# One-level Strassen products for the MLP up-projections of a two-layer trunk, with the MLP split into an up and a down phase

## The chip, the cores and the metric

The kernel is one program on one core of a Trainium2 chip. The metric is device time in microseconds (us). Before the change three runs took 2766.5, 2768.09 and 2774.47 us, median 2768.09. TensorE is PE in the profile (its weight loads PEld), VectorE is DVE, ScalarE is ACT, GpSimd is POOL, and SP is the engine that issues most loads.

## The reference

A sequence of 1024 tokens with 1024 features goes through two layers. Layer 0 mixes tokens by retention, layer 1 by a state-space block (S5). After each mixer comes the same MLP, and everything is float32:

```python
def conv_ffn(h, w_up, conv_w, conv_b, w_down):        # D_FF = 2816
    val, gate = jnp.split(h @ w_up, 2, axis=-1)       # (1024 x 1024) @ (1024 x 5632)
    gate = causal_depthwise_conv(gate, conv_w, width=3) + conv_b
    return (jax.nn.silu(gate) * val) @ w_down
h = rms_norm(x) * (1.0 + sc2) + sh2
x = x + g2 * conv_ffn(h, ...)
```

## The kernel before

Activations lie with features on the 128 partitions and tokens along the row. A float32 product is made of three reduced-precision ones (`mm3`): weight and activation are each split into a high part `hi` and a rest `lo`, and one bank of PSUM takes hi·hi, hi·lo and lo·hi. The split of a weight tile is one ACT copy (`hi`, L214) and one DVE subtraction (`lo`, L215).

A half is 512 of the 1024 tokens, and all matmuls of the MLP are 128x128 weights against 128x512 activations. The 2816 hidden features are 22 tiles. For each tile, `up` (L1352) makes gate and value for both halves, 8 blocks of the reduction each: 2 x 2 x 8 x 3 = 96 matmuls. `gate_out` copies the gate into the buffer `E`, `val_out` runs the convolution (one DVE `tensor_scalar`, two `scalar_tensor_tensor`), the silu on ACT, the product with the value (L1345), and splits the result again (L1349, L1350). After every two tiles the down-projection of the two tiles before them is added to `x` in SBUF (L1189). `lead` (L1363) begins an MLP: its first 96 matmuls need half 0 alone, while the normalisation of half 1 (`Norm.steps`) comes in piece by piece, block after block of the reduction.

Each engine executes its own queue in the order in which the Python code issues instructions. `W` (`Stream`) holds the weights in order of use: raw tiles (3 buffers), then hi and lo (5 buffers each). `pump` splits one tile ahead wherever it is called. `bg` takes one step of background work: in layer 0's MLP this is `s5_weights`, which prepares tables for S5, mainly on POOL, in 201 steps; 25 of them make eight groups of S5 (two half-blocks).

Of the kernel before, what the change touches and what calls it, by code (L numbers as in the profile page):

```python
# [18 lines left out]
P = 128  # L19
T = 1024  # L20
# [61 lines left out]
def trunk_kernel(ctx: ExitStack, tc: tile.TileContext, x, c, pos, ada_w, ada_b, ret_w_in, ret_w_out,  # L82
# [85 lines left out]
    NB = NFF // 2  # L168

    def ffn_list(l):  # L170
        wu, wd = ffn_w_up[l], ffn_w_down[l]
        for b in range(NB + 1):
            if b < NB:
                for ff in (2 * b, 2 * b + 1):
                    yield ("ug", l, ff), cols8(wu, FF + ff * P), 8
                    yield ("uv", l, ff), cols8(wu, ff * P), 8
            if b == NB:
                dn = range(2 * NB - 4, 2 * NB)
            elif 0 < b < NB - 1:
                dn = range(2 * b - 2, 2 * b)  # L180
            else:
                dn = ()
            for ff in dn:
                yield ("dn", l, ff), wd[ff * P:(ff + 1) * P, :].rearrange("p (o n) -> p o n", o=1), 1

    class Stream:
        RAW = 3
        BUFS = 5

        def __init__(self):  # L190
            self.items = list(weight_list())
            self.raw, self.hl = {}, {}
            self.nd = self.nsp = self.ng = self.use = 0

        def loads(self, upto=None):
            top = min(self.nsp + self.RAW, len(self.items))
            if upto is not None:
                top = min(top, upto)
            while self.nd < top:
                _, ap, k = self.items[self.nd]  # L200
# [4 lines left out]

        def split(self, later=None):
            i = self.nsp
            if i not in self.raw:
                self.loads()
            r = self.raw.pop(i)  # L210
            _, _, k = self.items[i]
            hi = w_p.tile([P, T], F32R, tag="whi", name="whi", bufs=self.BUFS)
            lo = w_p.tile([P, T], F32R, tag="wlo", name="wlo", bufs=self.BUFS)
            A.activation(out=hi, in_=r, func=AF.Copy)  # L214
            low = lambda: V.tensor_tensor(out=lo, in0=r, in1=f(hi), op=ALU.subtract)  # L215
            low() if later is None else later.append(low)
            self.hl[i] = (hi.rearrange("p (k n) -> p k n", k=k), lo.rearrange("p (k n) -> p k n", k=k))
            self.nsp += 1

        def get(self, key, n=1, more=False):  # L220
# [1606 lines left out]
```

## Time and profile before

| what | value |
|---|---|
| runs | 2766.5, 2768.09, 2774.47 us |
| span of the profiled execution | 2763.6 us |
| PE busy | 2701.4 us, 98% |
| DVE busy | 1568.2 us, 57% |
| ACT busy | 778.7 us, 28% |
| POOL busy | 769.4 us, 28% |
| DMA moved | 288.39 MB, mean 104 GB/s |

The span is from the first to the last instruction of one profiled execution; its own device time is not listed apart from the three runs, which are 2.9 to 10.9 us above the span (the median 4.5 us). Busy time of PE counts a stretch once, also where two matmuls overlap, so the mean duration of a matmul is not the time that it adds; the starts in the timeline tell that. Layer 0's MLP is from about 920 to 1680 us, layer 1's from about 2026 us to the end.

### The profile page before, as it was taken

What the parts mean: (1) busy time and instruction counts of PE and PEld (TensorE: products, weight loads), DVE (VectorE), ACT (ScalarE), POOL (GpSimd) and SP (SyncE); (2) the same over time, 40 slices, a digit from 0 to 9 for tenths busy, and PEclk for the clock granted to TensorE, in tenths of its full rate; (3) what the DMA queues carried; (4) which work ended last, traced back from release to release, by engine and by line L of the source; (5) the groups of instructions that cost most, each with busy time, mean ns of one, the idle gap of its engine ahead of it and who ended that gap; (6) DMA issues with size and microseconds to landing.
All of it is one profiled execution on the core that took longest, in us unless ns stands there. A gap on an engine that the chain in (4) does not pass through costs nothing.

```text
span 2763.6 us, 33159 instructions
## 1 busy us (share of the span) xinstructions
PE 2701.4 (98%) x13305; PEld 2274.2 (82%) x13305; DVE 1568.2 (57%) x2149; ACT 778.7 (28%) x1210; POOL 769.4 (28%) x631
## 2 busy tenths in 40 slices
PE   6999999999999999999999999999999999999999
PEld 5798888888888788888887888888888888888888
DVE  8664664745765776665566445772265445454444
ACT  5322131231322333333333224222232222222222
POOL 5356576775101323333333013220110000000004
PEclk8999999999999999999999999999999999999999
DMA  7544335353431132333233215983111111111111
GB/s 243 162 134 143 120 114 163 116 159 100 146 130 61 37 106 92 99 98 99 92 97 97 66 46 167 310 271 114 54 39 54 46 54 50 51 54 46 46 39 62
DMA packets 292069, 288.39 MB, mean 104 GB/s; under 512 B 37292, under 2 KB 248780, under 8 KB 291916
## 3 DMA queue, kind: packets, MB, share of 16 engines
q1 hardware_dynamic: 259276, 239.47, 28.4%
q10 hardware_dynamic: 32640, 46.82, 4.8%
q8 instruction: 104, 1.70, 0.3%
q14 instruction: 49, 0.40, 0.0%
HBM read 229.94 MB, written 54.69 MB: 103 GB/s over the span
## 4 chain that ended last, share of the span: by engine, by line
PE 82%; DVE 8%; ACT 3%; DMA 2%; issue 2%; POOL 2%; SPq 1%; ACTq 0%; POOLq 0%; DVEq 0%
PE bk L485 25%; PE bk L487 25%; PE bk L486 25%; PE bk L797 1%; PE bk L795 1%; PE bk L796 1%; PE bk L1529 1%; POOL ar L128 1%; DVE stf L870 1%; DMA blk<-in_ada_w 1%; DVE wlo L215 1%; PE bk L891 1%; ACT whi L214 1%; DVE gve L857 1%; ACT sth L871 0%
## 5 line engine op out<-in xcount | busy, mean ns | idle before, releaser
L485 PE MATMUL bk<-hh,whi 128*128 128x512 f32 x2048 | 805.8, 393 | 6.2 <-DVE t L1345 2.5
L486 PE MATMUL bk<-hl,whi 128*128 128x512 f32 x2048 | 801.1, 391 | 5.4 <-POOL hl L128 2.6
L487 PE MATMUL bk<-hh,wlo 128*128 128x512 f32 x2048 | 800.3, 391 | 0.3 <-DVE wlo L215 0.3
L215 DVE TENSOR_TENSOR wlo<-wr,whi 128x1024 fp32r<-128x1024 f32 x220 | 299.2, 1361 | 401.9 <-ACT whi L214 401.2
L485 PEld LDWEIGHTS bk<-hh,whi 128*128 128x128 f32 x2048 | 386.6, 189 | 89.4 <-DVE t L1345 2.9
L486 PEld LDWEIGHTS bk<-hl,whi 128*128 128x128 f32 x2048 | 386.5, 189 | 88.0 <-POOL hl L128 5.7
L487 PEld LDWEIGHTS bk<-hh,wlo 128*128 128x128 f32 x2048 | 386.3, 189 | 81.5 <-DVE wlo L215 0.7
L1189 DVE SCALAR_TENSOR_TENSOR x<-bk,mods,x 128x512 f32<-128x512 f32 x352 | 275.7, 801 | 167.7 <-PE bk L487 167.5
L485 PE MATMUL bk<-fh,whi 128*128 128x512 f32 (+1 forms) x736 | 281.8, 383 | 0.8 <-DVE t L1345 0.8
L214 ACT ACTIVATE whi<-wr 128x1024 fp32r<-128x1024 f32 x220 | 231.0, 1055 | 176.4 <-PE bk L486 132.4
L486 PE MATMUL bk<-fl,whi 128*128 128x512 f32 (+1 forms) x736 | 279.6, 380 | 0.0
L487 PE MATMUL bk<-fh,wlo 128*128 128x512 f32 (+1 forms) x736 | 279.6, 380 | 0.0
L1782 POOL TENSOR_SCALAR xn<-xn,prm 128x256 f32<-128x256 f32 (+1 forms) x21 | 11.6, 555 | 656.4 <-ACT facc L1774 656.4
L1331 ACT ACTIVATE E<-bk 128x512 f32<-128x512 f32 x88 | 52.5, 597 | 443.1 <-PE bk L487 429.0
L311 POOL TENSOR_TENSOR aacc<-aacc,ar 128x1024 f32<-128x1024 f32 x70 | 173.3, 2476 | 5.8
L485 PEld LDWEIGHTS bk<-fh,whi 128*128 128x128 f32 x736 | 138.2, 188 | 28.6 <-DVE t L1345 1.2
L128 POOL TENSOR_TENSOR nacc<-nacc,ar 128x512 f32<-128x512 f32 x36 | 46.6, 1294 | 410.9 <-ACT ar L403 410.7
L487 PEld LDWEIGHTS bk<-fh,wlo 128*128 128x128 f32 x736 | 138.2, 188 | 26.4
L486 PEld LDWEIGHTS bk<-fl,whi 128*128 128x128 f32 x736 | 138.2, 188 | 25.8
L128 POOL TENSOR_TENSOR ar<-sp 128x512 f32<-128x512 f32 (+1 forms) x64 | 82.7, 1308 | 246.0 <-ACT sev L1121 127.3
L1345 DVE TENSOR_TENSOR t<-t,bk 128x512 f32<-128x512 f32 x88 | 60.5, 687 | 156.6 <-PE bk L487 94.2
L795 PE MATMUL bk<-whi,hh 128*128 128x256 f32 x512 | 147.2, 288 | 0.0
(279 smaller groups left out, 4133.7 us busy)
## 6 DMA issues: line engine op xcount, KB each, us to landing
wr<-in_ffn_w_up SPq DMA_DIRECT2D x88, 512.0 KB, 3.8
ar<-in_ada_w SPq DMA_DIRECT2D x80, 512.0 KB, 4.5
wr<-in_ret_w_in SPq DMA_DIRECT2D x48, 512.0 KB, 4.0
wr<-in_ffn_w_down SPq DMA_DIRECT2D x44, 512.0 KB, 3.4
blk<-in_ada_w SPq DMA_DIRECT2D x32, 256.0 KB, 6.2
act_d<-sg ACTq DMA_DIRECT2D x16, 512.0 KB, 4.9
wr<-in_ret_w_out SPq DMA_DIRECT2D x16, 512.0 KB, 3.4
ar<-act_d SPq DMA_DIRECT2D x16, 512.0 KB, 3.3
```

What stands on the lines that cost most here:

```text
L128: GP.tensor_tensor(out=out, in0=in0, in1=in1, op=op)
L214: A.activation(out=hi, in_=r, func=AF.Copy)
L215: low = lambda: V.tensor_tensor(out=lo, in0=r, in1=f(hi), op=ALU.subtract)
L311: eng.tensor_tensor(out=acc, in0=acc, in1=raw, op=ALU.add)
L485: PE.matmul(bk, lhsT=lh, rhs=rh, start=first, stop=False)
L486: PE.matmul(bk, lhsT=lh, rhs=rl, start=False, stop=False)
L487: PE.matmul(bk, lhsT=ll, rhs=rh, start=False, stop=last)
L795: PE.matmul(o, lhsT=hh, rhs=wh[:, k % 4, :], start=(k == 0), stop=False)
L796: PE.matmul(o, lhsT=hh, rhs=wl[:, k % 4, :], start=False, stop=False)
L1189: V.scalar_tensor_tensor(out=dst, in0=bk, scalar=g, in1=src, op0=ALU.mult, op1=ALU.add)
L1331: A.activation(out=e[:, 2:10, hf * 64:(hf + 1) * 64], in_=b3, func=AF.Copy)
L1345: V.tensor_tensor(out=s_, in0=s_, in1=bk, op=ALU.mult)
```

## The change

Per hidden tile the value and gate weights are cut into quarters: A11 and A12 are the value weights of the first and last 512 inputs, A21 and A22 the gate weights. The activations are cut into B11, B21 (half 0, first and last 512 inputs) and B12, B22 (half 1). Instead of eight block products there are seven, of 4 x 3 = 12 matmuls each (84 per tile), in the order A11·B11, S2·T2, S3·T3, S1·T1, A22·T4, A12·B21, S4·B22, with S1 = A21+A22, S2 = S1-A11, S3 = A11-A21, S4 = A12-S2, T1 = B12-B11, T2 = B22-T1, T3 = B22-B12, T4 = B21-T2.

- The weight sums S1 to S4 are four POOL instructions per tile (`sums`). Each of the seven quarter weights is split by its own ACT copy and DVE subtraction of 128x512, one at each `pump`.
- The activation sums T1 to T4 and their splits are made at the start of each MLP by `steps_s`, on DVE and ACT.
- Products share banks: A22·T4 is added onto the bank of S3·T3 after that was read, A12·B21 onto that of A11·B11, S4·B22 onto that of S1·T1. The outputs are assembled by DVE additions (L1126).
- The first four tiles (`lead`) take their value of half 0 in one go of 96 matmuls; their five other products follow. The other 18 tiles have seven products each.
- The first multiplication of the convolution moves from DVE to ACT. The MLP's activations go to DRAM (`ff_d`) and come back in the down phase, which begins when all 22 tiles are done and works in groups of 4, 4, 4, 3, 3 and 4 tiles. `x` waits in DRAM meanwhile.
- In layer 0 the 201 background steps are taken one per product in the 18 full tiles and then two per column block in the down phase.

On PE the program has 528 rows fewer than before. On DVE, in layer 1, this stands for one half of one tile before: `E` is the gate, `t1` the convolution, `t2` the product, `fl` the rest of its split; the last row splits a weight tile that is used two tiles later.

```order
L1341 TENSOR_SCALAR t1_15422<-E_15418,prm_113 128x512
L1342 SCALAR_TENSOR_TENSOR t1_15422<-E_15418,prm_113,t1_15422 128x512 [waits DVE_49]
L1343 SCALAR_TENSOR_TENSOR t1_15422<-E_15418,prm_113,t1_15422 128x512 [waits DVE_49]
L1345 TENSOR_TENSOR t2_15423<-t2_15423,bk_16200 128x512 [waits PE_49,Activation_49]
L1350 TENSOR_TENSOR fl_16231<-t2_15423,fh_16230 128x512 [waits Activation_49]
L215 TENSOR_TENSOR wlo_16237<-wr_16070,whi_16236 128x1024 [waits DMAHW6_49,Activation_49]
```

The same engine and layer now, in a full tile from the end of its product A22·T4. Of the two L296 rows the first is the split of A11 and the second that of S2, both of the next tile; `tu` is the partial sum.

```order
L1126 TENSOR_TENSOR E_15613<-tu_15617,bk_16317 128x8x64 [waits PE_49]
L1549 SCALAR_TENSOR_TENSOR t1_15615<-E_15613,prm_113,t1_15615 128x512 [waits DVE_49,Activation_49]
L1550 SCALAR_TENSOR_TENSOR t1_15615<-E_15613,prm_113,t1_15615 128x512 [waits DVE_49]
L296 TENSOR_TENSOR wlo_16392<-wr_16333,wlo_16392 128x512 [waits DMAHW2_49,Activation_49]
L1549 SCALAR_TENSOR_TENSOR t1_15615<-E_15613,prm_113,t1_15615 128x512 [waits Activation_49]
L1550 SCALAR_TENSOR_TENSOR t1_15615<-E_15613,prm_113,t1_15615 128x512 [waits DVE_49]
L1126 TENSOR_TENSOR t2_15616<-t2_15616,bk_16282 128x512 [waits DMAHW1_49,PE_49]
L296 TENSOR_TENSOR whi_16413<-wr_16333,whi_16413 128x512 [waits Activation_49]
L1126 TENSOR_TENSOR tu_15617<-tu_15617,bk_16336 128x512 [waits PE_49]
```

A weight's split stands now between evacuations, two products before its use; each product's weights are split at the place of the second product before it.

At the start of layer 0's MLP the normalisation of half 1 stood like this on DVE before: per block `k` one product with the row scale (L441 or L438) and one split (L450 or L448).

```order
L441 TENSOR_TENSOR ar_7625<-x0_6527,bk_7840 128x512 [waits PE_49,Pool_49]
L438 SCALAR_TENSOR_TENSOR ar_7625<-x1_6566,mods_114,bk_7840 128x512
L450 CAST hh_7643<-ar_7625 128x8x64 [waits Activation_49]
L441 TENSOR_TENSOR nx_7626<-x2_6636,bk_7840 128x512 [waits Pool_49]
L448 SCALAR_TENSOR_TENSOR hl_7670<-ar_7625,mods_114,hh_7669 128x8x64 [waits Activation_49]
```

Now, from the last T4 on, after 40 other instructions (the first product with the row scale of half 1 counted as number 1): L639 makes T4, L600 splits it and the four B22, and the L296 row is the split of S1 of tile 0 (number 47), followed by the evacuation of S2·T2, the split of A22 (number 49) and that of S3·T3.

```order
L639 TENSOR_TENSOR ht_7920<-hf_7774,ht_7920 128x512 [waits Activation_49]
L600 TENSOR_TENSOR hs_7975<-ht_7920,hs_7975 128x512 [waits Activation_49]
L600 TENSOR_TENSOR hs_7978<-hl_7855,hs_7978 128x512 [waits Activation_49]
L600 TENSOR_TENSOR hs_7981<-hl_7860,hs_7981 128x512 [waits Activation_49]
L600 TENSOR_TENSOR hs_7984<-hl_7898,hs_7984 128x512 [waits Activation_49]
L600 TENSOR_TENSOR hs_7987<-hl_7915,hs_7987 128x512 [waits Activation_49]
L296 TENSOR_TENSOR whi_8003<-aacc_7742,whi_8003 128x512 [waits PE_49,Activation_49]
L1126 TENSOR_TENSOR tu_7741<-tu_7741,bk_7990 128x512 [waits PE_49]
L296 TENSOR_TENSOR wlo_8020<-wr_7618,wlo_8020 128x512 [waits Activation_49]
L1126 TENSOR_TENSOR E_7737<-tu_7741,bk_8007 128x8x64 [waits DVE_49,PE_49]
```

What came in piece by piece now stands as one block in front of the weights of the third product.

The core of the diff:

```diff
+    Q7 = ("A11", "S2", "S3", "S1", "A22", "A12", "S4")
+    Q5 = ("S2", "S3", "S1", "A22", "S4")
     class Stream:
         RAW = 3
-        BUFS = 5
+        RING = 5
...
+        def sums(self, i, which):
...
+            if which == "S1":
...
+                gp_tt(self.tmp, a21, a22, ALU.add)
+                gp_tt(a21, a11, a21, ALU.subtract)
+            elif which == "S2":
+                gp_tt(a11, self.of[first], a11, ALU.subtract)
+            else:
+                gp_tt(a12, a12, a11, ALU.subtract)
...
+                hi, lo = t[:, 0:HW], t[:, HW:T]
+                A.activation(out=hi, in_=src, func=AF.Copy)
+                V.tensor_tensor(out=lo, in0=src, in1=f(hi), op=ALU.subtract)
...
+                if q in ("A22", "S4"):
+                    self.used += 1
+                    self.raw.pop(first + (q == "S4"))
+                self.nsp += 1
                 self.loads()
+                self.ready(i + 1)
...
         def pump(self):
             self.loads()
-            if self.nsp < min(self.ng + self.BUFS - self.use, len(self.items)):
+            if self.can():
                 self.split()
...
+        def product(bk, w, act, first, last=True):
+            hi, lo = w
+            for k in range(4):
+                mm3(bk, hi[:, k, :], lo[:, k, :], act[k][0], act[k][1], first and k == 0, last and k == 3, True)
...
+            A.activation(out=a3, in_=E[:, 2:10, cs], func=AF.Copy, scale=w2_)
...
+        def pair(ff, val0=None, u=None, after=lambda i: None):
...
+            def next_(i):
+                W.pump()
+                bg(1)
...
+            b2 = new_bank()
+            product(b2, q("S2"), SB.t2, True)
+            next_(1)
+            tt(u, u, b2, ALU.add)
...
+            b4 = new_bank()
+            product(b4, q("S3"), SB.t3, True)
+            next_(2)
+            g1 = E[:, 2:10, 64:128]
+            tt(g1, as_sel(u, chalf), as_sel(b4, chalf), ALU.add)
...
+            product(b4, q("A22"), SB.t4, False)
+            next_(4)
+            tt(E[:, 2:10, 0:64], as_sel(u, chalf), as_sel(b4, chalf), ALU.add)
+            free_bank(b4)
+            small(0)
+            conv(ff, 0)
...
+        us, v0, uu, vv = lead()
+        W.tmp = sq[:, 0, :]
+        for i in range(3):
+            nrm.step(4)
+            W.pump()
+        nrm.flush()
+        for ff in range(LEADS):
+            pair(ff, vv[ff], uu[ff])
...
+                SP.dma_start(out=raw[ff], in_=f_d[ff])
+                yield
+                hi, lo = take(F32R, "fh"), take(F32R, "fl")
+                A.activation(out=hi, in_=raw[ff], func=AF.Copy)
+                V.tensor_tensor(out=lo, in0=raw[ff], in1=f(hi), op=ALU.subtract)
...
+        def last(i):
...
+            for _ in range(2):
+                if len(xin) < 8 and len(free) > 3:
+                    k = len(xin)
+                    xin.append(take(F32, f"x{k}"))
+                    SP.dma_start(out=xin[k], in_=x_d[k])
+            if i > 0:
+                next(pre)
+                next(pre)
+
+        pair(NFF - 1, after=last)
```

## Rows read from the trace of the kernel before

**Rows 1.** The page, busy time and share of each engine.
```profile
PE 2701.4 (98%) x13305; PEld 2274.2 (82%) x13305; DVE 1568.2 (57%) x2149; ACT 778.7 (28%) x1210; POOL 769.4 (28%) x631
```

**Rows 2.** Waits of PE inside the MLPs: for whom, us in total, times, longest.
```profile
PE bk L485 <- DVE t L1345: 3.3, 2, 2.5
```

**Rows 3.** Groups of PE instructions by line and shape: count | busy us, mean ns | idle.
```profile
L485 PE MATMUL bk<-hh,whi 128*128 128x512 f32 x2048 | 805.8, 393 | 6.2 <-DVE t L1345 2.5 <-ACT hh L650 1.6 <-DVE rtmp L781 1.4
...
L485 PE MATMUL bk<-fh,whi 128*128 128x512 f32 x672 | 262.9, 391 | 0.8 <-DVE t L1345 0.8
```

**Rows 4.** Timeline of PE in layer 1's MLP: start us, duration us, instruction.
```profile
2304.40 0.39 PE L485 MATMUL bk<-hh,whi 128*128 128x512 f32 x1
2304.63 0.39 PE L486 MATMUL bk<-hl,whi 128*128 128x512 f32 x1
2304.86 0.39 PE L487 MATMUL bk<-hh,wlo 128*128 128x512 f32 x1
```

**Rows 5.** Timeline of DVE and ACT there: convolution, silu, product and split.
```profile
2301.02 0.27 ACT L1333 ACTIVATE E<-bk 128x126 f32<-128x126 f32 x1
...
2310.02 0.75 DVE L1342 SCALAR_TENSOR_TENSOR t<-E,prm,t 128x512 f32<-128x512 f32 x1
...
2310.81 0.75 DVE L1343 SCALAR_TENSOR_TENSOR t<-E,prm,t 128x512 f32<-128x512 f32 x1
...
2311.66 0.72 ACT L1344 ACTIVATE t<-t,prm 128x512 f32<-128x512 f32 x1 [3.32 <-DVE t L1343]
...
2312.41 0.69 DVE L1345 TENSOR_TENSOR t<-t,bk 128x512 f32<-128x512 f32 x1 [0.85 <-ACT t L1344]
...
2313.14 0.63 ACT L1349 ACTIVATE fh<-t 128x512 fp32r<-128x512 f32 x1 [0.75 <-DVE t L1345]
...
2313.80 0.69 DVE L1350 TENSOR_TENSOR fl<-t,fh 128x512 fp32r<-128x512 f32 x1 [0.70 <-ACT fh L1349]
```

**Rows 6.** Groups of ACT at the end of the span: a copy scaled by a column.
```profile
L1756 ACT ACTIVATE nat<-bk,rs 128x512 f32<-128x512 f32 x8 | 5.3, 675 | 2.2 <-POOL rs L1745 2.2
```

**Rows 7.** Timeline of DVE at the start of layer 0's MLP.
```profile
941.35 0.69 DVE L441 TENSOR_TENSOR ar<-x,bk 128x512 f32<-128x512 f32 x1 [6.25 <-PE bk L423]
941.96 0.74 DVE L438 SCALAR_TENSOR_TENSOR ar<-x,mods,bk 128x512 f32<-128x512 f32 x1
...
953.94 2.87 DVE L1341 TENSOR_SCALAR t<-E,prm 128x512 f32<-128x512 f32 x1
956.84 1.66 DVE L1342 SCALAR_TENSOR_TENSOR t<-E,prm,t 128x512 f32<-128x512 f32 x1
958.54 1.42 DVE L1343 SCALAR_TENSOR_TENSOR t<-E,prm,t 128x512 f32<-128x512 f32 x1
```

**Rows 8.** Stretch after a wait of PE: us, busy by engine (instructions), granted clock, DMA.
```profile
961.40:964.50 3.10, 3.01 (x7) 2.44 (x8) 2.33 (x5) 0.63 (x1) 0.00 (x0) 0.50 0.00 0
```

**Rows 9.** One line's durations, min/median/max ns: layer 0's MLP twice, then layer 1's.
```profile
L1342 DVE SCALAR_TENSOR_TENSOR t<-E,prm,t x32: 750/752/1802, 988.9 to 1500.4; 128x512 f32<-128x512 f32 x32
...
L1345 DVE TENSOR_TENSOR t<-t,bk x33: 686/687/689, 981.6 to 1503.5; 128x512 f32<-128x512 f32 x33
...
L1342 DVE SCALAR_TENSOR_TENSOR t<-E,prm,t x42: 750/751/754, 2058.0 to 2680.2; 128x512 f32<-128x512 f32 x42
```

**Rows 10.** Layer 0's MLP: busy by engine; then two DVE groups of it.
```profile
980.00:1540.00 560.00, 556.51 (x2524) 453.54 (x2523) 339.77 (x420) 192.30 (x287) 181.08 (x176) 1.00 0.31 97
...
L1342 DVE SCALAR_TENSOR_TENSOR t<-E,prm,t 128x512 f32<-128x512 f32 x32 | 30.8, 962 | 1.2
L1115 DVE SCALAR_TENSOR_TENSOR sev<-ar,sev 128x512 f32<-128x512 f32 x32 | 27.2, 849 | 10.6 <-POOL ar L1107 10.1
```

**Rows 11.** Groups of POOL: an addition of 128x512, the nearest to the weight sums.
```profile
L128 POOL TENSOR_TENSOR nacc<-nacc,ar 128x512 f32<-128x512 f32 x36 | 46.6, 1294 | 410.9 <-ACT ar L403 410.7
```

**Rows 12.** DMA issues (count, KB each, median us to landing); a stretch with much DMA.
```profile
wr<-in_ffn_w_up SPq DMA_DIRECT2D x88, 512.0 KB, 3.8
...
30.00:40.00 10.00, 6.95 (x12) 3.28 (x12) 9.86 (x8) 6.19 (x8) 8.20 (x5) 0.52 1.10 349
```

More of the change, by code (lines that the diff above doesn't have):

```diff
@@ L204, in loads, with ring, quarter @@
                 self.nd += 1
+        def ring(self, tag):
+            assert self.out[tag] < self.RING, (tag, self.nsp)
+            self.out[tag] += 1
+            return w_p.tile([P, T], F32R, tag=tag, name=tag, bufs=self.RING)
+        def quarter(self, i):
+            _, q, first, qs = self.items[i]
+            if q == "S1":
+                return self.of[first]
+            r = self.raw[first + (q in ("A11", "A12", "S2", "S4"))]
+            return r[:, HW:T] if q in ("A12", "A22", "S4") else r[:, 0:HW]
@@ new lines, in ready, with can @@
+        def ready(self, i):
+            if i < len(self.items) and self.items[i][1] != "w" and self.tmp is not None:
+                _, q, first, qs = self.items[i]
+                if first + 1 < self.nd:
+                    if q == qs[0]:
+                        self.sums(i, "S1")
+                    if q == "S2":
+                        self.sums(i, "S2")
+                    if q == "S4":
+                        self.sums(i, "S4")
+        def can(self):
+            if self.nsp >= len(self.items):
+                return False
+            _, q, first, _ = self.items[self.nsp]
+            if q == "w":
+                if self.extra(self.nsp):
+                    return self.spare > 0 and len(free) > 1
+                return max(self.out.values()) < self.RING
+            return self.tmp is not None and self.out[("whi", "wlo")[self.turn]] < self.RING
@@ new lines, in lead @@
+            us = take(F32, "us")
+            v0 = [take(F32, "v0") for _ in range(2)]
+            uu = [tu[:, 0, :], tu[:, 1, :], us[:, 0:HW], us[:, HW:T]]
+            vv = [t[:, i * HW:(i + 1) * HW] for t in v0 for i in range(2)]
+            for kp in range(0, KT, 2):
+                for i, (bk, (wh, wl)) in enumerate(zip(bks, ws)):
+                    for k in (kp, kp + 1):
+                        mm3(bk, wh[:, k, :], wl[:, k, :], SB.b1[k][0], SB.b1[k][1], k == 0, k in (3, 7), True)
+                    if kp == 2:
+                        A.activation(out=uu[i], in_=bk, func=AF.Copy)
+                nrm.step(3)
@@ L1389, in down_mm, with feed @@
+        pair(NFF - 1, after=last)
+        store()
+        drop(tmp)
+        W.tmp = None
+        while len(xin) < 8:
+            k = len(xin)
+            xin.append(take(F32, f"x{k}"))
+            SP.dma_start(out=xin[k], in_=x_d[k])
+        xs[:] = xin
+        W.spare = 3
+        def feed(ff):
+            while ff not in acts:
+                next(pre)
         def down_mm(ws, ffs, m, hf):
@@ L1396, in down_mm @@
             return bk
-        lead()
-        for b in range(NB - 2):
-            up(b + 1)
-            ffs = (2 * b, 2 * b + 1)
-            ws = W.get(("dn", l, ffs[0]), 2)
+        for a_, b_ in GROUPS[:-1]:
+            ffs = tuple(range(a_, b_))
+            ws = W.get(("dn", l, a_), b_ - a_)
+            feed(b_ - 1)
             for m in range(8):
```

392 lines of the change are left out of this document (280 added, 112 removed).

## The prediction

> **What bounds the kernel now.** I read the page's busy shares first: PE 98%, DVE 57%, ACT and POOL 28% [rows 1]. Then the waits of PE: inside the MLPs they come to a few microseconds, the longest one 2.5 [rows 2]. So the length of PE's queue is the time, and a change that shortens it gains exactly that, as long as the others still keep up. Then the price of a matmul. The groups give a mean of 393 ns [rows 3], but the timeline shows one starting every 0.227 us [rows 4]: neighbours overlap. The price of one more or less is 0.227 us, and a saving counted with 393 would be 1.7 times too large. Last I read how DVE and ACT do one tile [rows 5], since the change gives them more work in less time.
>
> **What goes.** A tile has 84 matmuls instead of 96: 22 x 12 x 2 layers = 528 fewer, 528 x 0.227 = 119.9 us. The up matmuls now read contiguous rows; the down matmuls did so before and take 391 ns beside 393 [rows 3], so I give nothing for it. The down phase has the same matmuls; that DVE adds to x 96 times a layer instead of 160 lies beside PE, worth 0. A product of 12 matmuls is 2.72 us, a full tile 19.05 us.
>
> **What a full tile adds.** Weights are split two products ahead, in DVE's queue behind the evacuations of the products before, so a late DVE makes PE wait for weights. The longest chain begins when A22·T4 ends: DVE's addition into E 0.69; ACT's small copy 0.27 [rows 5] and scaled copy, by the nearest row 0.68 [rows 6]; two STT 1.5; silu 0.72; ACT's hi of the next tile's A11, which stands in its queue before the next scaled copy, 0.63; that copy 0.68; two STT 1.5; silu 0.72; hi of S2 0.63, lo 0.69 [rows 5]. That is 8.7 us. One thing comes on top: POOL makes S2 in place of A11, so it may begin only when A11's lo is done, which is when the two STT run. L1342, with both operands in SBUF, takes 750 ns alone and up to 1802 in the stage where POOL works, while L1345, with one operand in PSUM, never leaves 686 to 689 [rows 9]. So I charge one POOL addition, 1.2 (1.29 in [rows 11]). Hops of 0.04 to 0.10 [rows 5] make some 0.2 net of ACT's overlaps: 10.1 us. The product's third matmul is the first to need lo, 0.45 later than its start: 9.65. PE meanwhile has A12, S4 and A11, 3 x 2.72 = 8.16. It waits 1.5 us per tile (bounds 0, if the meeting doesn't happen, and 2.7, if POOL holds DVE twice). 17 tiles in layer 1: 26 us. Behind that wait on DVE stand the last two additions of the tile and the splits of S3 and S1, which are just in time.
>
> **Layer 0 adds the background work.** POOL was busy 181 us with it [rows 10]; 126 of its 201 steps fall into 18 full tiles: 6.3 us a tile, beside 4 x 1.2 of sums. DVE's part is 27 us for L1115 [rows 10] and about as much for its other steps, 2 us a tile. Before, L1342 grew from 752 to a mean of 962 there [rows 9, 10] with POOL busy 32%. Eight such DVE instructions lie on the chain: 8 x 0.21 = 1.7. Of the work of DVE and ACT that is queued into the chain I take 0.6, and 0.5 for S3's weights, which then come late. 1.5 + 2.8 = 4.3 us a tile (bounds 2 and 8), 17 tiles: 73 us.
>
> By the Trainium skill ("SBUF — State Buffer", section "Who interferes with whom") a DVE instruction with two SBUF inputs and a GpSimd instruction that reads SBUF exclude each other for their whole length. The two lines of [rows 9] agree with it.
>
> **What the start of each MLP adds.** The row scale of half 1 reaches PE after 72 of the 96 first matmuls, so PE has 24 left, 5.4 us. Before, DVE normalised block by block and PE followed. Now DVE does 46 instructions before the split of S1's weights, the third product's. At 0.62 us from start to start, as 941.35 to 941.96 [rows 7], number 47 ends after 29.1 us; PE could have come there after 5.4 + 2 x 2.72 = 10.9, so it waits 18 us. Then a second chain: the buffer of the next tile's value weights is free only after the split of A22 (number 49, 30.4 us). Then the load, 3.8 [rows 12]; two POOL sums, 2.4; hi and lo of S2, 1.3. This split stands on DVE before the addition into E, which so comes at 38 instead of 16.5 us: 21.5 late. The next two lead tiles have the same loop: from E, 8.3 to the second next split, 3.4 to that of A22, 3.8 + 2.4 + 1.3 and hops, 19.5 us beside 13.6 of PE: 2 x 5.9. The fourth goes over into full tiles, whose first product needs no sum: 5.5. Together 39 us per MLP (bounds 28 and 48). Two times, less 5.5 us of waits that were there: 72 us.
>
> **What the end of the up phase adds.** During the last tile, 19 us, eight tiles of x, six of activations and four of weights are loaded: 18 x 0.524 = 9.4 MB, 27 us at the 349 GB/s of [rows 12]. On ACT each activation's hi waits for its load, and behind it in the queue stand the copies, silus and weight splits of the running tile; the first down product needs four weights split behind all that. I take 16 us a layer (bounds 8, the transfers alone, and 28, one behind another): 32. The other loads and stores of activations are 0.5 MB per tile each and lie beside PE; free.
>
> After a wait of PE before 961.4 the granted clock was 0.50, the lower of its two levels (1.2 GHz), for the next 3 us [rows 8]. The new waits of this length will do so too: 3 at 1.7 us, 5.
>
> The sum: -119.9 + 26 + 73 + 72 + 32 + 5 = +88 on the profiled span of 2763.6: 2852. The median of the runs is 4.5 above that span, so I forecast about **2855 us**, slower.
>
> **Rivals.** (1) Faster: the product count decides. If DVE and ACT keep the chain of a full tile under 8.2 us, because POOL makes S2 before the STT come, and the background steps fall between the chains, the tiles cost nothing and the start and the end remain at their lower parts: -120 + 50 + 16 + 34 = -20, 2748; with all tiles free 2714. It turns on the 1.5 us per tile, which is a small difference of two large sums. For it: DVE has only 13 us of instructions in a tile of 19. Against it: they are tied to ACT, one by one, in a fixed order. (2) Still slower: in layer 0 DVE and POOL are full together. A tile has 12 DVE instructions with two SBUF operands, 8.5 us; with the background's 2 and POOL's 6.3 + 4.8 that is 21.6 us when one excludes the other, where PE needs 19 to 20; what is then out of step comes on top, 8 us a tile: +63, 2918. By the skill's rule named above this is the floor of a tile in layer 0; by the extension of 0.21 us alone it isn't reached. (3) The change could fail to remove work from PE: its queue has 528 rows fewer, so I give this none. (4) Gains and losses cancel within 0.3%, the least that a measurement of this kernel can tell from no change: 2760 to 2776.
>
> **How the numbers follow.** Forecast 0.64, own range 2785 to 2920; rival 1 0.15; rival 2 0.17; rival 4 0.04. The low bounds of all terms together give 2763.6 - 120 + 0 + 34 + 50 + 16 + 4.5 = 2748, the high ones 2763.6 - 120 + 46 + 136 + 91 + 56 + 10 + 4.5 = 2987; that all are high at once is unlikely, so 2750 to 2945. Nearly all of rival 1 lies below 2760: faster 0.14, within 0.3% 0.04, slower 0.82.
>
> **What would show it.** In the profile after: PE's share well under 98%; its waits headed by the weight splits (L295 and L296) and by DVE's normalisation at the start; 18 to 40 us without a busy PE after the first 96 matmuls of each MLP; the full tiles of layer 1 some 20.5 us apart, those of layer 0 about 24; L1549 above 751 ns wherever POOL works; a gap at the change to the down phase, with ACT waiting for a load. I am wrong if tiles come every 19 us in layer 1, or if the start costs under 20 us: then weights or normalisation were ready although their place in the queue says otherwise.

## The result, and the profile after

The changed kernel takes 2975.28 us (median of 4 runs, 2971.31 to 2981.27) beside 2770.03 for the kernel before in the same series: a ratio of 1.0743, 95% interval 1.0725 to 1.0762. That is slower, as forecast, but by 205 us and not by 85: it lies above the range (2750 to 2945). The profiled execution has a span of 2979.5 us, 215.9 more than before; the forecast had 88.

The page's busy shares answer [rows 1]:
```profile
PE 2695.0 (90%) x12777; PEld 2214.2 (74%) x12777; DVE 1761.8 (59%) x2369; ACT 927.7 (31%) x1486; POOL 999.3 (34%) x797
```
528 instructions of PE are gone as counted (13305 to 12777), but its busy time fell by 6 us, not by 120. So PE's remaining matmuls have become longer. The page's costliest groups of PE say the same: the up matmuls took 393 ns on average in [rows 3].
```profile
L681 PE MATMUL bk<-hs,whi 128*128 128x512 f32 x648 | 273.3, 422 | 110.2 <-ACT whi L295 103.6
L681 PE MATMUL bk<-hs,wlo 128*128 128x512 f32 x584 | 241.5, 414 | 55.1 <-ACT wlo L295 53.5
...
L683 PE MATMUL bk<-fh,wlo 128*128 128x512 f32 (+1 forms) x544 | 210.3, 387 | 0.3 <-DVE wlo L283 0.2
```
The up products (`hs`) show 405 to 422 ns, the down products (`fh`) 387 to 393 as before. The idle time ahead of them, by the waits of PE over the whole span (us in total, times, longest):
```profile
PE bk L681 <- ACT whi L295: 103.6, 33, 13.4
PE bk L681 <- ACT wlo L295: 53.5, 28, 4.8
PE bk L1307 <- POOL ar L128: 16.4, 4, 9.9
PE bk L1329 <- POOL ar L128: 12.2, 5, 4.1
PE bk L681 <- DVE tu L1126: 11.7, 1, 11.7
```
[rows 2] had 3.3 us as its largest entry inside the MLPs. L295 is the hi of a weight quarter, as forecast; L1307 and L1329 are matmuls of layer 0's background work, which the forecast did not name; all nine of their waits stand in its down phase.

The stretches of the two MLPs, up and down phase each (us, busy time of PE, PEld, DVE, ACT, POOL, then PE's granted clock), answer [rows 8, 10]:
```profile
922.10:1543.20 621.10, 499.00 (x1984) 378.99 (x1985) 403.74 (x503) 247.44 (x419) 253.58 (x212) 0.90 0.30 99
1543.20:1839.00 295.80, 267.05 (x1144) 215.37 (x1145) 147.94 (x172) 79.62 (x96) 84.71 (x82) 0.93 0.35 118
2188.90:2715.80 526.90, 456.59 (x1865) 356.39 (x1863) 332.08 (x448) 195.91 (x353) 125.72 (x94) 0.94 0.24 80
2715.80:2979.50 263.70, 254.27 (x1232) 213.61 (x1232) 133.03 (x162) 56.09 (x72) 30.02 (x42) 0.97 0.25 89
```
Layer 0's up phase takes 94 us longer than layer 1's, which has the same matmuls and no background. The spacing of full tiles is read from one instruction of the convolution, which stands twice in each, L1549 (it answers [rows 9]): durations min/median/max ns, first and last start from tile 4 to tile 20 (counted from 0), 16 tiles apart, in layer 0 and in layer 1:
```profile
L1549 DVE SCALAR_TENSOR_TENSOR t<-E,prm,t x33: 737/752/1871, 1080.0 to 1487.4; 128x512 f32<-128x512 f32 x33
...
L1549 DVE SCALAR_TENSOR_TENSOR t<-E,prm,t x33: 750/752/754, 2344.1 to 2677.6; 128x512 f32<-128x512 f32 x33
```
That is 25.46 us a tile in layer 0 and 20.85 in layer 1, where I forecast about 24 and 20.5. With these starts the stages can be held against PE's count (0.227 us a matmul):

| stage | forecast beyond PE's count | measured |
| --- | --- | --- |
| start, first matmul to tile 4's convolution: 396 matmuls and 1.7 us, 91.6 | 39 each | 157.9 and 155.2: 66 and 64 |
| full tiles of layer 1, against 19.05 | 1.5 each | 1.8 each |
| full tiles of layer 0, against those of layer 1 | 2.8 each | 4.6 each |
| end, tile 20's convolution to the first down product: 22.8 | 16 each | 55.8 and 38.2: 33 and 15 |
| down phases | 0 | 38 in layer 0, about 6 in layer 1 |

### The profile page after: what moved, and what is told of

The parts are those of the page before. It is cut to its first block, busy times and chain, and to the rows that moved or that the text cites. A ratio compares the mean times of both kernels' runs of the same rounds, so it can differ in the third digit from the quotient of the medians.

```text
span 2979.5 us, 33406 instructions
## 1 busy us (share of the span) xinstructions
PE 2695.0 (90%) x12777; PEld 2214.2 (74%) x12777; DVE 1761.8 (59%) x2369; ACT 927.7 (31%) x1486; POOL 999.3 (34%) x797
## 4 chain that ended last, share of the span: by engine, by line
PE 55%; DVE 20%; ACT 10%; DMA 6%; POOL 4%; issue 4%; SPq 1%; ACTq 1%; POOLq 0%; DVEq 0%
PE bk L681 16%; PE bk L683 16%; PE bk L682 16%; DVE t L1550 3%; DVE t L1549 2%; DVE wlo L296 2%; POOL ar L128 2%; DVE whi L296 2%; ACT t L1551 2%; DVE E L1126 1%; ACT t L1548 1%; ACT wlo L295 1%; POOL wr L128 1%; DMA fr<-ff_d 1%; ACT whi L295 1%
## 5 line engine op out<-in xcount | busy, mean ns | idle before, releaser
L681 PE MATMUL bk<-hs,whi 128*128 128x512 f32 x648 | 273.3, 422 | 110.2 <-ACT whi L295 103.6
L681 PE MATMUL bk<-hs,wlo 128*128 128x512 f32 x584 | 241.5, 414 | 55.1 <-ACT wlo L295 53.5
L683 PE MATMUL bk<-hs,wlo 128*128 128x512 f32 x648 | 266.6, 411 | 4.9 <-DVE wlo L296 4.6
L682 PE MATMUL bk<-hs,whi 128*128 128x512 f32 x648 | 266.9, 412 | 2.2 <-POOL hs L128 1.7
L283 DVE TENSOR_TENSOR wlo<-wr,whi 128x1024 fp32r<-128x1024 f32 x128 | 180.5, 1414 | 134.9 <-ACT whi L282 134.9
L681 PE MATMUL bk<-hh,whi 128*128 128x512 f32 x640 | 254.2, 397 | 3.9 <-ACT hh L846 1.7
L682 PE MATMUL bk<-hl,whi 128*128 128x512 f32 x640 | 252.5, 395 | 3.0 <-POOL hl L128 2.1
L683 PE MATMUL bk<-hh,wlo 128*128 128x512 f32 x640 | 251.9, 394 | 0.2 <-DVE wlo L283 0.2
L683 PE MATMUL bk<-hs,whi 128*128 128x512 f32 x584 | 243.5, 417 | 2.2 <-DVE whi L296 1.7
L681 PEld LDWEIGHTS bk<-hs,whi 128*128 128x128 f32 x648 | 130.1, 201 | 152.0 <-ACT whi L295 118.7
L682 PE MATMUL bk<-hs,wlo 128*128 128x512 f32 x584 | 236.5, 405 | 0.0
L128 POOL TENSOR_TENSOR wr<-wr 128x512 f32<-128x512 f32 x88 | 118.3, 1344 | 333.5 <-DVE whi L296 148.7
L681 PEld LDWEIGHTS bk<-hs,wlo 128*128 128x128 f32 x584 | 115.0, 197 | 90.7 <-ACT wlo L295 65.8
L683 PEld LDWEIGHTS bk<-hs,wlo 128*128 128x128 f32 x648 | 127.5, 197 | 48.0 <-DVE wlo L296 21.6
L296 DVE TENSOR_TENSOR wlo<-wr,wlo 128x512 fp32r<-128x512 f32 x124 | 108.2, 872 | 79.4 <-ACT wlo L295 79.4
```

Source lines behind the costliest of these rows:

```text
L128: GP.tensor_tensor(out=out, in0=in0, in1=in1, op=op)
L296: V.tensor_tensor(out=lo, in0=src, in1=f(hi), op=ALU.subtract)
L681: PE.matmul(bk, lhsT=lh, rhs=rh, start=first, stop=False, skip_group_check=skip)
L682: PE.matmul(bk, lhsT=lh, rhs=rl, start=False, stop=False, skip_group_check=skip)
L683: PE.matmul(bk, lhsT=ll, rhs=rh, start=False, stop=last, skip_group_check=skip)
```

## The experiments

All times stand against the kernel before, run on the same chip; tile times are spacings of the same convolution instruction from tile 4 to tile 20. The changed kernel was timed in another series; the kernel before took 2765.3 to 2770.0 us in these series, so differences of under 5 us from the changed kernel tell nothing by themselves, and the argument goes by the stages.

**Look-ahead.** Two more weight quarters are split before the full tiles begin.
```
+        for _ in range(2):
+            W.pump()
         for ff in range(LEADS, NFF - 1):
             pair(ff)
```


> Two more weight quarters are split before the loop of full tiles begins, so that in every full tile the splits run four products ahead of PE instead of two; nothing else changes. My theory: a full tile is longer than its matmuls because the splits stand behind the evacuations and the convolution on DVE and ACT, and PE waits for whi and wlo. Then the full tiles of layer 1 come every 19.0 to 19.4 us instead of 20.85, and the waits of PE on L295 and L296 in them go; layer 0's tiles shrink by 2 us or more each from 25.5; together 50 to 80 us less. Rival A: DVE and ACT have no time left in a tile (throughput), or the banks of PSUM come free too late; then the look-ahead only moves the waits and layer 1 stays at 20.8, the total within 5 us of the changed kernel. Rival B, for layer 0 alone: POOL's background steps are what is short there; then layer 1 falls to 19.2 and layer 0 stays above 24.

2978.98 us, ratio 1.0756 (1.0725 to 1.0787). The convolution's instruction, layer 0 and layer 1:
```profile
L1549 DVE SCALAR_TENSOR_TENSOR t<-E,prm,t x33: 743/752/1539, 1085.1 to 1499.0; 128x512 f32<-128x512 f32 x33
...
L1549 DVE SCALAR_TENSOR_TENSOR t<-E,prm,t x33: 750/751/754, 2354.0 to 2668.2; 128x512 f32<-128x512 f32 x33
```
Layer 1: 19.64 us, a little over the 19.0 to 19.4 expected: what held its tiles is how late the splits stand, as the forecast's chain has it. Layer 0: 25.87, no gain. There another thing is short, and the waits of PE say which: in the changed kernel and in this run,
```profile
PE bk L681 <- DVE E L1126: 1.5, 2, 1.3
```
```profile
PE bk L681 <- DVE E L1126: 94.7, 32, 10.5
```
65.6 of these us stand ahead of A22·T4 in layer 0's full tiles: PE may add to the bank of S3·T3 only when DVE has read it. DVE stands behind a split there, ACT's hi of that split behind one of POOL's weight sums: ACT's waits at L295 for them are 63.3 us between tiles 4 and 20 of layer 0, and 3.7 in the changed kernel. In layer 1, where POOL has no background in its queue, PE's waits ahead of A22·T4 are 15.0. This fits rival B. The last tiles grew (47 and 40 us), so the total did not fall.

**Background out of the way.** `bgq.append(behind)` is moved from ahead of the full tiles to behind the up phase, with `bg_drain()` right after it.

> Layer 0's background work (the weights of the S5 mixer, made by POOL, DVE, ACT and a few PE transposes) isn't run in the full tiles and the down phase, but drained at once between the two phases. My theory: background steps and the half clock that follows their waits make a full tile of layer 0 longer than one of layer 1 (25.5 beside 20.85 us). Then layer 0's tiles come every 20.9 us with no wait on L128 in them, 74 us less over 16 tiles; the down phase is 35 us shorter, about 263 us; in between stand some 200 us in which the background runs alone, so the kernel as a whole is slower by about 90 us. Rival: layer 0's tiles are longer for another reason (the store of x, the loads of weights, the state of the clock); then they stay above 23 us without any background.

3219.68 us, ratio 1.1625 (1.159 to 1.166). Layer 0's tiles:
```profile
L1549 DVE SCALAR_TENSOR_TENSOR t<-E,prm,t x33: 751/752/753, 1075.3 to 1409.1; 128x512 f32<-128x512 f32 x33
```
20.87 us, the time of layer 1, and the down phase takes 255.7. So the 4.6 us a tile are the background's, all of them. Alone between the phases it needed some 380 us (the up phase grew to 903.8 us, beside 525.5 in layer 1), not 200. The engines then work nearly one after another: in the 385 us from 1440 to 1825, PE is busy for 50, DVE 80, ACT 81 and POOL 163.

**Interleaved subtractions.** T4's subtraction goes between the splits of T3.
```
 for i in range(4):
     V.tensor_tensor(out=low[i], in0=high[i], in1=low[i], op=ALU.subtract)
+for i in range(4):
     parts(low[i], S.t3)
     S.lh.put(low[i])
+    V.tensor_tensor(out=t2[i], in0=S.f[i + 4], in1=t2[i], op=ALU.subtract)
...
```


> In the normalisation of the second half, the eight subtractions that make T3 and T4 no longer all stand ahead of the splits: each is followed by a split, so ACT makes a hi while DVE subtracts. My theory: DVE's queue of about 46 instructions is the start, and the un-interleaved part costs 2.0 us per block instead of 1.24. Then the stretch from the row scale to the split of S1's weights falls from 36.5 to about 30.5 us, PE's waits at the start of each MLP by 5 to 6 us, the total by 10 to 14 us. Rival: the start is set by the loop of value weights (load, POOL sums, split, addition into E); then DVE ends earlier but the lead tiles still come every 20.5 us, and the total changes by less than 4 us.

2965.05 us, ratio 1.0706 (1.0675 to 1.0737), 10 less than the changed kernel; the first convolution comes 67.0 and 66.0 us after the MLP's first matmul instead of 73.1 and 74.2. DVE in the changed kernel, layer 1 (start, duration, instruction; the last field is idle time and what ended it):
```profile
2213.43 2.48 DVE L590 TENSOR_TENSOR hl<-x,bk 128x512 f32<-128x512 f32 x4 [6.34 <-PE bk L585]
...
2233.92 0.69 DVE L600 TENSOR_TENSOR hs<-hl,hs 128x512 fp32r<-128x512 f32 x1 [0.70 <-ACT hs L596]
2234.53 0.68 DVE L634 TENSOR_TENSOR hl<-hl 128x512 f32<-128x512 f32 x1
2235.91 0.69 DVE L600 TENSOR_TENSOR hs<-hl,hs 128x512 fp32r<-128x512 f32 x1 [0.69 <-ACT hs L596]
...
2249.89 0.69 DVE L296 TENSOR_TENSOR whi<-aacc,whi 128x512 fp32r<-128x512 f32 x1
...
2260.31 1.21 DVE L296 TENSOR_TENSOR wlo<-wr,wlo 128x512 fp32r<-128x512 f32 x1 [4.50 <-ACT wlo L295]
2261.44 0.68 DVE L1126 TENSOR_TENSOR E<-tu,bk 128x512 f32<-128x512 f32 x1
```
and with the subtractions interleaved:
```profile
2203.41 2.48 DVE L590 TENSOR_TENSOR hl<-x,bk 128x512 f32<-128x512 f32 x4 [6.34 <-PE bk L585]
...
2219.93 2.49 DVE L634 TENSOR_TENSOR hl<-hl 128x512 f32<-128x512 f32 x4
...
2224.14 0.68 DVE L600 TENSOR_TENSOR hs<-hl,hs 128x512 fp32r<-128x512 f32 x1
2224.74 0.69 DVE L638 TENSOR_TENSOR ht<-hf,ht 128x512 f32<-128x512 f32 x1
2225.35 0.69 DVE L600 TENSOR_TENSOR hs<-hl,hs 128x512 fp32r<-128x512 f32 x1
...
2233.54 0.69 DVE L296 TENSOR_TENSOR whi<-aacc,whi 128x512 fp32r<-128x512 f32 x1
```
The split of S1's weights ends 37.2 us after the row scale in the first and 30.8 in the second. The forecast of 0.62 us an instruction from [rows 7] (29.1 in all) supposed that DVE never waits; a block of T3 or T4 took 1.99 instead of 1.24, because DVE subtracts, ACT makes the hi, and DVE stands until it is there. Interleaved, the price holds.

**One reload step per product** in the last tile, where there were two:
```
             if i > 0:
                 next(pre)
-                next(pre)
```


> In the last tile of the up phase the reload of the activations advances by one step per product instead of two: a load is issued at one product and split at the next, and ACT no longer waits for a load it has just issued. My theory: at the end of the up phase ACT waits for the loads, and PE behind it for weights. Then the last tile falls from 42.9 to 30 to 35 us in layer 0 and from 29.5 to 22 to 25 in layer 1, while up to 5 us come back at the start of the down phase, since fewer activations are ready; total 8 to 15 us less. Rival: the loads themselves (9.4 MB at 349 GB/s, 27 us) are what is late; then what the tile gains comes back as a wait ahead of the first down product, and the total stays within 3 us.

2971.29 us, ratio 1.0728 (1.0694 to 1.0762), 4 less, between the theory (8 to 15) and the rival (within 3). The last tile took 24.6 and 20.5 us instead of 42.9 and 29.5, the up phases were 11.1 and 9.9 us shorter, but the down phases 8.4 and 5.7 us longer. In the changed kernel, between 1488 and 1545 us:
```profile
ACT fh L1658 <- DMA fr<-ff_d: 17.7, 2, 16.9
```
ACT waited for a load whose issue stood just before it, as the theory says; once it doesn't, most of the time comes back in the down phase, as the rival says. By the stages 7 us of the end are the order. That the rest is the transfers was not shown.

**Sums that overwrite nothing fresh.** S2 goes into the free half of S1's buffer, S4 into A11's place.
```
-                gp_tt(a11, self.of[first], a11, ALU.subtract)
+                gp_tt(self.tmp[1], self.tmp[0], a11, ALU.subtract)
...
-                gp_tt(a12, a12, a11, ALU.subtract)
+                gp_tt(a11, a12, self.of[first][1], ALU.subtract)
```


> POOL's sums no longer overwrite a quarter that has just been split: S2 goes into a half tile of its own (the unused half of the buffer of S1) as soon as the raw weights are there, and S4 goes into A11's place, whose split is long past. The number of instructions is the same. In the changed kernel POOL stands 8 us per layer-0 tile behind L296 (131.6 us in 410), and L1550 takes 1207 ns in layer 1 beside 752 of L1549, because the held sum runs just then. Theory Q (queues): in layer 0 the sums hold POOL's queue, the background steps behind them come late, and ACT and DVE, which issue those steps' other halves in order, stand still with the split and the convolution behind them. Then layer 0's tiles fall by 2 us or more from 25.5, and those of layer 1 by 0.5 to 1.2 from 20.85, with L1550 near 760 ns. Theory P (shared access to SBUF): what counts is how long POOL works while DVE wants two SBUF operands, wherever it stands; then layer 0 stays within 1 us of 25.5 and only layer 1 gains a little.

2968.24 us, ratio 1.0723 (1.0691 to 1.0754). Full tiles: 25.49 and 20.86 us, unchanged; theory Q in this form fails. POOL's waits for L296 in layer 0's tiles fell as meant, and nobody was faster for it. L1550 (L1547 in this run) still takes 1209 ns in layer 1, so a sum still meets the second multiplication of the convolution, and the share that this meeting has in layer 1's tiles was not taken apart. Only the first lead tiles gained (20.4 and 20.4 to 18.9 and 19.2 us in layer 0), where S2 is now made ahead of S3.

**POOL work without a dependence, in layer 1.**
```
+                if dm is not None and val0 is None:
+                    gp_tt(dm[:, 0:384], dm[:, 0:384], dm[:, 512:896], ALU.add)
...
```


> Layer 1, which has no background work, gets some without any dependence: after each product of a full tile POOL adds 128x384 elements of a scratch tile, 7 times about 1 us per tile, as much as the background's POOL time per tile in layer 0 (6.9 us). The scratch adds compute nothing that is used. Theory P (shared access): DVE's instructions with two SBUF operands stretch as in layer 0 (L1549 from 752 to 950 or more), and the tile grows from 20.85 to 22.5 or more, most of the way to layer 0's 25.5. Theory Q (queues: ACT, PE and DVE stand in order behind background steps that wait for POOL): the tile grows by less than 0.8, since nothing waits for these adds.

2994.81 us, ratio 1.0819 (1.0787 to 1.085). Layer 1's tiles:
```profile
L1549 DVE SCALAR_TENSOR_TENSOR t<-E,prm,t x33: 750/915/939, 2334.0 to 2685.0; 128x512 f32<-128x512 f32 x33
```
21.94 us, 1.1 more, between both theories: POOL's mere work costs something, but less than a quarter of 4.6.

**Matmuls in PE's waits**, or just ahead of them: in tiles 1 to 3 PE has no wait ahead of S2, and the next one is ahead of S3.
```
+            fill(b2, 50 if ff == 0 else 16 if ff < LEADS else 6 if l == 0 else 0)
             product(b2, q("S2"), SB.t2, True)
```


> Matmuls whose result is overwritten stand where PE waits: at tile 0 of each MLP 50 ahead of the S2 product, 12 ahead of S3 and 16 ahead of S1, 16 ahead of S2 in tiles 1 to 3, and 6 ahead of S2 in each full tile of layer 0. They add 126 + 108 in layer 0 and 126 in layer 1 to the queue, but are meant to lie inside waits. Theory: part of what the start and layer 0's tiles cost is that PE runs at half clock after each wait (121 us of half clock in layer 0's up phase, 58 in layer 1's). Then the half clock falls below 60 and 35 us, layer 0's tiles from 25.5 to about 24, the time from the MLP's first matmul to the fifth tile by 5 us or more, and the total by 20 to 40 us. Rival: the waits end at a moment that DVE and ACT set, and slower matmuls only fill the waits; then the half clock goes but the stages keep their length within 3 us, and the total changes by less than 10 us either way.

2971.97 us, ratio 1.0736 (1.0705 to 1.0767). The two up phases:
```profile
920.40:1539.90 619.50, 536.60 (x2219) 413.78 (x2219) 404.28 (x503) 247.64 (x419) 253.05 (x212) 0.94 0.30 100
2180.90:2704.80 523.90, 474.68 (x1991) 372.02 (x1989) 332.23 (x448) 195.91 (x353) 125.71 (x94) 0.98 0.24 80
```
The time at the lower of PE's two clock levels (1.2 GHz, granted clock 0.50) fell from 121 to 74 us and from 58 to 20, the mean granted clock rose from 0.90 to 0.94 and from 0.94 to 0.98, and the phases are 1.6 and 3.0 us shorter. In layer 0 that is less than the fall to 60 that I expected, but the starts show it best: up to tile 4 the time at the lower level fell from 54.5 to 20.4 and from 47.7 to 10.2 us, a wait of 0.8 us or more is left behind every filled place, so the filling held nobody up, and the starts took 158.9 and 152.2 us instead of 157.9 and 155.2. The rival holds: the slow matmuls fill time that DVE and ACT set. (In layer 0's full tiles 11 of the 18 fillings left no wait behind them, so these tiles, 25.43 us, say less.)

**The background's halves.** The real background runs behind the up phase, as above; the tiles hold an echo of one half of it.

> The real background of layer 0 runs between the phases, where it delays nobody in the tiles (20.85 us each then); in the full tiles stand only its POOL instructions once more, at the same places, with results that nobody uses, and none of its PE, DVE and ACT instructions. So the tiles show what POOL's work alone costs. By the scratch adds in layer 1, which cost 1.1 us a tile, I expect 21.7 to 22.5 us; if POOL's work is what makes a tile of 25.5, 24 or more.

> The other half: the real background between the phases, and in layer 0's full tiles its PE, DVE, ACT and DMA instructions once more at the same places, on data that nobody uses, without the POOL instructions. If the instructions of DVE (2.8 us a tile) and ACT and their waits for PE and for each other are what lengthens a tile, 23 to 24.5 us; if they are harmless as long as POOL isn't late, below 22. If this and the POOL half sum to less than the 4.6 us, the rest is the waiting of ACT and DVE for POOL.

3249.7 and 3254.8 us, one run each. Layer 0's tiles with POOL's half, then with the rest:
```profile
L1622 DVE SCALAR_TENSOR_TENSOR t<-E,prm,t x33: 751/752/1724, 1073.2 to 1434.6; 128x512 f32<-128x512 f32 x33
```
```profile
L1654 DVE SCALAR_TENSOR_TENSOR t<-E,prm,t x33: 740/751/840, 1077.1 to 1444.8; 128x512 f32<-128x512 f32 x33
```
22.59 us (+1.7; a little over the range) and 22.98 (+2.1; at its lower edge). They make 3.8 of 4.6; 0.8 is left for what the halves do to each other, the waits between them among it.

**Finer background steps.** The ACT half of a step is issued one product after its PE, DVE or POOL half, at four places like this:
```
                     PE.transpose(bk[:, g * P:(g + 1) * P], ta[:, g * P:(g + 1) * P], ident)
+                yield
                 A.activation(out=ev0, in_=bk, func=AF.Copy)
```


> The background's steps are cut finer: the ACT copies of what PE has transposed or multiplied, the ACT sines of DVE's angle and the stores of POOL's sums are issued one step (one product) after their producers instead of with them; same instructions. In the changed kernel ACT stands for about 60 us in layer 0's full tiles at such background results, with splits and convolutions behind it. If these waits make the tile, layer 0's tiles fall from 25.5 to 23.5 or less and the total by 25 to 40 us; if it is DVE's added work itself, they stay above 24.8 and the total within 8 us.

2971.68 us, ratio 1.0744 (1.0721 to 1.0767). Layer 0's tiles take 24.68 us, 0.8 less, as much as is left above, and between what I expected of the two theories. But 16 steps were added in all, and the down phase grew to 304 us. The waits that this takes away are the smaller part, as the halves say.

**One background step per product in the down phase.**
```
-                    tick(2)
+                    tick()
```


> One change: behind each product of the down phase one background step instead of two. The 201 steps still fit (126 in the full tiles, 80 in the down phase). If two steps at once are what costs, because the pause that the steps leave for POOL is gone and PE's transposes wait for it, the down phase of layer 0 falls from 296 to 255 to 262 us, the waits of PE at L1307 and L1329 from 28 to under 8 us, the total by 33 to 40. If it is the amount of background left at that point, what is spread here comes back at the end of the phase, and it stays above 280.

2936.76 us, ratio 1.0619 (1.0598 to 1.064), 38 less than the changed kernel. The down phase of layer 0 and the waits of PE in it:
```profile
1540.20:1798.00 257.80, 254.54 (x1145) 206.71 (x1145) 146.63 (x172) 80.20 (x96) 86.91 (x82) 0.99 0.39 135
```
```profile
PE bk L1329 <- POOL ar L128: 2.1, 1, 2.1
PE bk L1307 <- POOL ar L128: 0.8, 2, 0.6
```
PE is busy 99% of it, with the same background, spread; without any background (above) the phase took 255.7.

**POOL helps at the start**, on top of the interleaved subtractions:
```
-                    parts(t1, S.t1)
+                    parts(t1, S.t1, pool=True)
...
-                parts(low[i], S.t3)
+                parts(low[i], S.t3, pool=i % 2 == 1)
```


> On top of the interleaved subtractions: POOL, idle at that moment, makes the lo of the four T1 blocks and of two T3 blocks, 6 of DVE's 46 instructions ahead of S1's split. If the number of DVE's instructions is the start, it gets 3.5 to 4.5 us shorter per MLP beside the run with interleaved subtractions alone (first L1549 at 66 to 67 us after the MLP's first matmul, then 62 to 63), 7 to 9 us in all. If POOL's work holds DVE up as it did in the tiles (L1549 975 instead of 752 ns) or ACT's hi parts are the pace, the gain is under 1.5 us per MLP.

2976.22 us, ratio 1.0762 (1.074 to 1.0783), 11 more than with interleaving alone: the help took all of that gain back. The split of S1's weights ends 37.9 us after the row scale again, and the first convolutions come at 74.0 and 73.2 us. DVE, then POOL, in layer 1's start:
```profile
2218.11 1.36 DVE L600 TENSOR_TENSOR hs<-ht,hs 128x512 fp32r<-128x512 f32 x1 [0.85 <-ACT hs L596]
...
2231.67 5.68 DVE L634 TENSOR_TENSOR hl<-hl 128x512 f32<-128x512 f32 x4
...
2250.56 0.68 DVE L296 TENSOR_TENSOR whi<-aacc,whi 128x512 fp32r<-128x512 f32 x1
```
```profile
2217.63 1.29 POOL L128 TENSOR_TENSOR hs<-ar,hs 128x512 fp32r<-128x512 f32 x1 [9.49 <-ACT hs L596]
...
2232.95 1.59 POOL L128 TENSOR_TENSOR wr<-wr 128x512 f32<-128x512 f32 x1
2234.62 1.59 POOL L128 TENSOR_TENSOR wr<-aacc,wr 128x512 f32<-128x512 f32 x1
```
POOL's instruction ends at 2218.92; DVE's, started at 2218.11 and 0.69 long by itself, ends at 2219.47, 0.55 after it. Four subtractions that take 2.49 together with the subtractions interleaved and POOL at rest take 5.68 beside POOL's sums.

**Combinations.** The first: the separate sums, look-ahead, interleaving, one reload step, one background step.

> Together: sums that overwrite nothing fresh, the look-ahead of two more quarters in the full tiles, the subtractions of T3 and T4 between the splits, one reload step per product in the last tile, and one background step instead of two behind each product of the down phase. By the parts measured so far: 10 us from the start, 14 from the two ends of the up phase, 20 from layer 1's tiles; by theory Q 30 to 60 more from layer 0's tiles and 20 from layer 0's down phase: 2850 to 2890. By theory P layer 0's tiles stay above 24.5 and the total above 2905.

2904.96 us, ratio 1.0494 (1.0464 to 1.0524). Layer 0's tiles stayed at 25.3 us; the separate sums cost layer 1's tiles 1 us against look-ahead alone (20.59). The second has them in the lead tiles only, and the finer steps:

> The better parts together: look-ahead of two more quarters in the full tiles, S2 ahead of S3 in a buffer of its own in the lead tiles only, in place elsewhere, subtractions of T3 and T4 between the splits, one reload step per product in the last tile, one background step per product in the down phase, and the finer background steps. Against the combination at 2905: layer 1's tiles 19.6 instead of 20.6 us, 16 less; layer 0's tiles as in the run with finer steps alone, 0 to 30 less. 2860 to 2890, still slower than the kernel before, since the two starts (about 60 us each) and layer 0's background stay.

2906.62 us, ratio 1.0511 (1.0494 to 1.0529): tiles of 24.54 and 19.74 us, but 290 us in layer 0's down phase, where the added steps end in a drain. The third is the second without the finer steps:

> The combination of all parts that helped, without the finer background steps: layer 0's up phase about 600 us, its down phase 255, layer 1 about 495 and 262. 2875 to 2885, the best so far and still 3.8 to 4.3% slower than the kernel before.

2896.35 us, ratio 1.0475 (1.0458 to 1.0493). Down phase 256, layer 1 492 and 262 as expected; layer 0's up phase 615 instead of 600, because its tiles took 26.1 us with look-ahead, as they took 25.9 with look-ahead alone. It is the fastest version with seven products that was run, 79 us under the changed kernel and some 130 above the kernel before.

## Why the prediction was right or wrong

**Direction and bound: right.** The product count did not decide. Layer 1's tiles meet the forecast (20.85 for 20.5), their cause is shown by the look-ahead, and the waits are headed by L295. In layer 1 they stand ahead of S2, as forecast (18 waits, 20.5 us), though at its first matmul, for ACT's hi, and not at the third, for DVE's lo. In layer 0 they stand ahead of A11 as well (19.5 us, beside 30.3 ahead of S2), which the forecast had not.

The forecast missed the added span by 128 us (216 for 88). By the sum below 52 of them are the start, 44 the down phases, 16 the end and 12 layer 0's tiles.

**The start: mis-sized, 39 forecast, 66 and 64 measured.** The 25 us between them have three parts, in layer 1's numbers. (a) "At 0.62 us from start to start ... number 47 ends after 29.1 us": it was 37.2, and interleaving showed why; with it the addition into E came 48.0 us after the row scale instead of 38: 10 us. (b) The 72 matmuls ahead of the row scale, which I took to run freely, needed 24.5 us (2188.9 to 2213.4) for 16.3: 8 us, of which 1.6 are sixteen small matmuls of the normalisation that stood there before too. (c) The lead tiles and the change to full tiles took 24 us beyond PE's count for 17: 6.5 us; a loop of 20.5 us where 19.5 was forecast, and a third one that I had left out. Nor does the wait stand ahead of S1's product alone: 13.0 us of it are ahead of S2's, the first, 3.1 ahead of S3's and 4.6 ahead of S1's.

**Layer 0's tiles: mis-sized, 2.8 forecast beyond layer 1, 4.6 measured.** About 1.1 of the 4.6 are the background's own matmuls, which the kernel before had as well; held against it, a tile lost 5.3 us where 4.3 was forecast. The part for POOL's work met its number, 1.7 forecast and 1.7 measured with POOL's half alone, but not by its working: the forecast had eight DVE instructions on the chain, each 0.21 longer, and its list of the chain has five of that kind. In the run, all 18 DVE instructions of a tile together grew by 2.0 us (13.7 to 15.7); how much of that lies on the chain was not measured. So the match is partly luck. The step that was too small is "of the work of DVE and ACT that is queued into the chain I take 0.6, and 0.5 for S3's weights": 1.1 for what the other half alone makes 2.1, and nothing for the 0.8 between the halves. Rival 2, DVE and POOL full together, isn't the cause: by the starts and ends in the trace both stand still for 3.9 of the 25.46 us of a tile, and POOL's half alone gives tiles of 22.6. What within the 2.1 is the length of the instructions and what their order was not taken apart.

**The down phase: the step that failed.** "The down phase has the same matmuls" gave 0. My own count left 75 of 201 background steps for that phase and never priced them. Two at once cost 38 us more than one at a time, which takes 2 more than a phase without background. The 6 us of layer 1's down phase are what is left of its MLP's excess when the other stages are taken off; their cause stays open.

**The end: 48 measured for 32,** 33 in layer 0, which is above its upper bound of 28, and 15 in layer 1. Of that about 7 us are the order of issue and split; what the rest is stays open.

**Half clock: the size was off, the price was not.** The up phases had 179 us at the lower level, far more than three stretches of 3. PE is busy for 122 of them, with matmuls 0.43 us apart instead of 0.227, so by estimate some 60 of the 114 us by which PE's busy time did not fall are theirs. But filling took away 86 of the 179 us and gave 5 back. That this is the size of the term is chance; that the price is small is shown.

By these terms the sum is -119.9 + 124.5 (start, less 5.5 that was there) + 29 + 85 (layer 0's tiles: 16 x 6.4 less about 1.1 each for the background's own matmuls, which were there before) + 48 + 44 = 211 of the 216 measured; the rest lies in the other stages.

DVE and POOL take turns: that is the rule of the Trainium skill ("SBUF — State Buffer", section "Who interferes with whom") that the prediction weighed, and the rows of the start with POOL's help agree with it to 0.14 us: 0.69 become 1.36, and by the rule DVE's instruction would end 0.69 after POOL's, where it ended 0.55 after. By it POOL is no reserve for DVE's work on two SBUF operands.

## What to carry to other kernels

Fewer matmuls are worth their time only if the engine that prepares their operands keeps pace: count its instructions, and add a wait for each pair in which it needs another engine's result at once, unless something stands between. Background work has to be priced in every stage that it falls into, by steps per product; the same steps one at a time cost 2 us where two at a time cost 40. Splitting weights earlier helps only until the engine that makes their sums is late: that was the look-ahead in layer 0. And a busy share of 90% did not mean that PE set the time: look at what lengthens a matmul before you believe it.

## What was not expected of the hardware

A third of the up phases' waits could be filled with matmuls and the granted clock raised from 0.90 to 0.94 and 0.94 to 0.98, for a gain of 1.6 and 3.0 us: a clock that is low between waits costs little as long as another engine sets when the next wait ends. And POOL is slowed by DVE as well as the other way round: its additions of 128x512 elements took 1.28 us alone and 1.59 to 1.72 among DVE's subtractions.
